# Delta rule: the small products issued in turns over the four quarters of the TensorE array

## The chip, the cores and the metric

One core of one Trainium2 chip runs the whole layer in one program. The metric is the device time of one execution in microseconds; several executions are made, and their median stands for the kernel.

## The reference, cut to what matters

A layer works on 512 latent tokens and 256 context tokens of width 1024. Three mixers read one input projection: a gated linear recurrence, the delta rule (RWKV-7 time mixing) and a neighbourhood attention. Then follow an output projection, a router, and 32 experts of which each token takes 4. The change touches the delta rule alone. It runs in both directions over the tokens, with 4 heads of 64 channels, and carries a 64 x 64 state per head:

```python
def _wkv7_scan(r, w, k, v, a_vec, b_vec, s0, reverse):
    def step(s, inp):
        r_t, w_t, k_t, v_t, a_t, b_t = inp
        sa = jnp.einsum('bhij,bhj->bhi', s, a_t)
        s = s * w_t[:, :, None, :] + sa[..., None] * b_t[:, :, None, :] + v_t[..., None] * k_t[:, :, None, :]
        return s, jnp.einsum('bhij,bhj->bhi', s, r_t)
```

Context tokens come first and give the latent tokens their starting state; only latent tokens give an output.

## The kernel before, in words

The delta rule is computed in chunks of 64 tokens. Six groups g of 128 tokens (two chunks c each) follow one another, g = 0 and 1 over the context, g = 2 to 5 over the latent tokens (`lat`); each is worked for both directions d. A unit is one head of one chunk: ct (2) and h (2) name the head, and a half of the 128 partitions holds one head or one chunk. All products are float32 with 64 rows of contraction and 64 output partitions, so each sits in one quarter of the 128 x 128 array: the half of its contraction rows and the half of its output partitions choose which. Each such product is two instructions on PE in the trace.

`early` (from L505) prepares a group: decays, keys, the products `ba` (L561), then two hops through DRAM and a loop of 15 steps on DVE that inverts the diagonal 16 x 16 blocks (tile M, L607 and L608). At its end it copies M, sends it to DRAM (L613) and reads it back as CX (L616).

`late` (from L621) then does, for one group and direction, a chain of steps with a `yield` after each: `tt` (transposes, L658), twice; `sc` (L672, L673 or L675), twice, once for each h; Y, kv, X, XT, Y, XT (all through `by_chunk`, L651), which complete the inverse of the chunk's matrix; `lv` (L712); `G` (L726 to L732), twice, once for each chunk c; `S` (L755, L757), twice, once for each chunk, which carries the state on. Every step writes one PSUM bank, and DVE or ACT then reads it out (evicts it). The four banks come from one pool that `late` of both directions and `early` share (psE and psR are the same pool of four, L1107). POOL makes X and XT from CX (L644) before the first Y can run.

In G before, a unit's products (3 for the context, 6 for the latent tokens) follow one another in one quarter; then comes the next unit. In `sc`, the two chunks alternate within one h, so two quarters take turns.

The order of the work: `rule` (L1142) takes one step each, in turn, of `late` for both directions and of `early` for the next group. `drive` (L1157) mixes three streams by rounds: two steps of `rule`, one step of `attention` (which starts after 12 idle rounds and has 97 steps left), and 0.22 steps of `modulations` (26 steps: products with the second part of ada_w, and biases). The tile framework then places each instruction on its engine's queue, by this order and by when its planner takes the inputs to be ready; a queue is worked in order. After the rule, `finish` (L767) normalizes its output, and `ahead` (L1177) fills PE with 24 products of the output projection (L1180), which need the attention's PSUM banks and output. Then come the rest of the output projection, the router, and the experts, whose weights stream from HBM.

Of the kernel before, what the change touches and what calls it, by code (L numbers as in the profile page):

```python
# [78 lines left out]
class Mixer:  # L79
# [541 lines left out]
    def late(self, g, d, lp, psR, u, st):  # L621


        nc, ident = self.nc, self.ident
        V, S_, P_, G_ = nc.vector, nc.scalar, nc.tensor, nc.gpsimd
        mm = P_.matmul
        lat = g >= 2
        XA, BK, PC, ba, CX = u['XA'], u['BK'], u['PC'], u['ba'], u['CX']
        bank = lambda nm: psR.tile([128, 512], F32, tag="b", name=nm)
        t_ = lambda nm, shape: lp.tile(shape, F32, tag=nm, name=nm)  # L630
        half = [slice(0, 64), slice(64, 128)]
        hv = lambda ap: ap[:, :256].rearrange("p (u t) -> p u t", u=4)
        units = [(ct * 2 + h, ct, h) for ct in range(2) for h in range(2)]
        TT = t_("TT", [128, 2, 5, 128])
        M3 = t_("M3", [128, 4, 3, 64])
        AM = t_("AM", [128, 2, 4, 64])
        X = t_("X", [128, 4, 64])
        XT = t_("XT", [128, 4, 64])

        def mask(j, msk):  # L640
            G_.tensor_tensor(AM[:, j], ba, msk.unsqueeze(1).to_broadcast([128, 4, 64]), op=ALU.mult)

        def blocks(w, dst):
            G_.tensor_tensor(dst.rearrange("p u (q t) -> p u q t", t=16), CX[:, w].unsqueeze(2).to_broadcast([128, 4, 4, 16]),  # L644
                             self.d16.rearrange("p (q t) -> p q t", t=16).unsqueeze(1).to_broadcast([128, 4, 4, 16]), op=ALU.mult)

        def by_chunk(b, lhsT, rhs, n=64):

            for hu, ct, h in units:
                for c in half:  # L650
                    mm(b[c, hu * n:(hu + 1) * n], lhsT(hu, c), rhs(hu, c), start=True, stop=True)  # L651

        mask(0, self.off16)
        blocks(0, X)
        for ct in range(2):
            b = bank("tt")
            for j, src in enumerate((XA[:, ct, 0, :], BK[:, ct, 0, :], BK[:, ct, 1, :], BK[:, ct, 2, :])):
                P_.transpose(b[:, j * 128:(j + 1) * 128], src, ident)  # L658
            S_.copy(TT[:, ct, 1:5, :], b.rearrange("p (j c) -> p j c", j=4))
            yield  # L660
            if ct == 0:
                blocks(1, XT)
        mask(1, self.off32)

        m3v = M3.rearrange("p (e h) v t -> p e h v t", h=2)
        for h, r in enumerate(half):
            b = bank("sc")
            bv = b[:, :384].rearrange("p (e v t) -> p e v t", e=2, v=3)
            for ct in range(2):
                for c in half:  # L670
                    if lat:
                        mm(bv[c, ct, 0, :], BK[r, ct, 0, c], XA[r, ct, 1, c], start=True, stop=True)  # L672
                        mm(bv[c, ct, 1:3, :], BK[r, ct, 1, c], XA[r, ct, :, c], start=True, stop=True)  # L673
                    else:
                        mm(bv[c, ct, 1, :], BK[r, ct, 1, c], XA[r, ct, 0, c], start=True, stop=True)  # L675
            if lat:
                V.tensor_tensor(m3v[:, :, h], bv, self.m3.unsqueeze(1).to_broadcast([128, 2, 3, 64]), op=ALU.mult)
            else:
                V.tensor_tensor(m3v[:, :, h, 1], bv[:, :, 1], self.m3[:, 1, :].unsqueeze(1).to_broadcast([128, 2, 64]), op=ALU.mult)
            yield  # L680
        b = bank("Y")
        by_chunk(b, lambda hu, c: AM[c, 0, hu, :], lambda hu, c: X[c, hu, :])
        Y = t_("Y", [128, 4, 64])
        S_.copy(Y, hv(b))
        yield
        b = bank("kv")
        by_chunk(b, lambda hu, c: M3[c, hu, 1, :], lambda hu, c: TT[c, hu // 2, 4, half[hu % 2]])
        S_.copy(TT[:, :, 0, :], b[:, :256].rearrange("p (c t) -> p c t", c=2))
        yield
        b = bank("X")  # L690
        by_chunk(b, lambda hu, c: XT[c, hu, :], lambda hu, c: Y[c, hu, :])
        V.tensor_tensor(X, hv(b), X, op=ALU.add)
        yield
        b = bank("XT")
        by_chunk(b, lambda hu, c: Y[c, hu, :], lambda hu, c: XT[c, hu, :])
        V.tensor_tensor(XT, hv(b), XT, op=ALU.add)
        yield
        b = bank("Y")
        by_chunk(b, lambda hu, c: AM[c, 1, hu, :], lambda hu, c: X[c, hu, :])
        Y = t_("Y", [128, 4, 64])  # L700
        S_.copy(Y, hv(b))
        yield
        b = bank("XT")
        by_chunk(b, lambda hu, c: Y[c, hu, :], lambda hu, c: XT[c, hu, :])
        V.tensor_tensor(XT, hv(b), XT, op=ALU.add)
        yield
        LV = t_("LV", [128, 2, 2, 128])
        b = bank("lv")
        bv = b.rearrange("p (c w h i) -> p c w h i", c=2, w=2, h=2)
        for hu, ct, h in units:  # L710
            for c in half:
                mm(bv[c, ct, :, h, :], XT[c, hu, :], TT[c, ct, 0:2, half[h]], start=True, stop=True)  # L712
        S_.copy(LV, b.rearrange("p (c w i) -> p c w i", c=2, w=2))
        yield

        L = t_("L", [128, 2, 2, 64])
        RT = t_("RT", [128, 2, 128]) if lat else None
        G = st['G']
        ys = []
        for c, k in enumerate(half):  # L720
            b = bank("G")
            bv = b.rearrange("p (w e t) -> p w e t", w=4, e=2)
            for ct in range(2):
                for n, h in enumerate(half):
                    hu = ct * 2 + n
                    mm(bv[h, 0, ct, :], LV[k, ct, 1, h], TT[k, ct, 2, h], start=True, stop=True)  # L726
                    mm(bv[h, 1, ct, :], TT[k, ct, 2, h], LV[k, ct, 0, h], start=True, stop=False)
                    mm(bv[h, 1, ct, :], TT[k, ct, 3, h], TT[k, ct, 4, h], start=False, stop=True)
                    if lat:
                        mm(bv[h, 2, ct, :], LV[k, ct, 1, h], M3[k, hu, 0, :], start=True, stop=True)  # L730
                        mm(bv[h, 3, ct, :], LV[k, ct, 0, h], M3[k, hu, 0, :], start=True, stop=False)
                        mm(bv[h, 3, ct, :], TT[k, ct, 4, h], M3[k, hu, 2, :], start=False, stop=True)  # L732
            V.tensor_tensor(G[c], bv[:, 0], self.i2.unsqueeze(1).to_broadcast([128, 2, 64]), op=ALU.add)
            V.tensor_tensor(L[:, c], bv[:, 1], PC[:, :, c:c + 1].to_broadcast([128, 2, 64]), op=ALU.mult)
            if lat:
                V.tensor_tensor(RT[:, :, k], bv[:, 2], XA[:, :, 1, k], op=ALU.add)
                q = (g - 2) * 128 + c * 64
                lo = q if d == 0 else NL - q - 64
                o = self.YD[:, :, lo:lo + 64]
                o = o[:, :, ::-1] if d else o  # L740
                ys.append(o)
                if g < 4:
                    S_.copy(o, bv[:, 3])
                else:
                    V.tensor_tensor(o, bv[:, 3], o, op=ALU.add)
            yield
        for c, k in enumerate(half):
            S, Sn = st['S'][st['n'] % 2], st['S'][(st['n'] + 1) % 2]
            b = bank("S")
            bv = b[:, :256].rearrange("p (w e t) -> p w e t", w=2, e=2)  # L750
            more = not (g == 5 and c == 1)
            for ct in range(2):
                for h in half:
                    if more:
                        mm(bv[h, 0, ct, :], G[c][h, ct, :], S[h, ct, :], start=True, stop=True)  # L755
                    if lat:
                        mm(bv[h, 1, ct, :], S[h, ct, :], RT[h, ct, k], start=True, stop=True)  # L757
            if more:
                for ct in range(2):
                    V.scalar_tensor_tensor(Sn[:, ct, :], bv[:, 0, ct, :], PC[:, ct, c:c + 1], L[:, c, ct, :], op0=ALU.mult, op1=ALU.add)  # L760
            if lat:
                V.tensor_tensor(ys[c], bv[:, 1], ys[c], op=ALU.add)
            st['n'] += 1
            yield
# [1389 lines left out]
```

## Time and profile before

| what | value |
|---|---|
| median of 3 runs | 1767.38 us (1763.82 to 1771.16) |
| the profiled execution, its own time | 1764.35 us |
| its span, first to last instruction | 1762.5 us |
| mean granted TensorE clock | 0.961 of full speed |
| busy, share of the span | PE 92%, PEld 51%, DVE 44%, ACT 28%, POOL 16% |
| data moved by DMA | 508.79 MB, 289 GB/s on average |

PE is the TensorE's products, PEld its weight loads, which overlap them; DVE, ACT and POOL are the vector, scalar and GpSimd engines, SP issues DMAs. Products overlap and their ends are modelled, so a busy PE is not always a PE at its peak. A line such as L726 is a line of the kernel. PEclk is the clock that the chip granted TensorE, 1.00 for 2.4 GHz; its other level is half of that. In rows of waits and in square brackets, `<-` names who released the wait.

### The profile page before, as it was taken

Reading aid. Unit: us, or ns where it says so; the run is one execution under the profiler, and the core shown is the slowest. Engines: PE = TensorE matmul, PEld = TensorE weight load, DVE = VectorE, ACT = ScalarE, POOL = GpSimd, SP = SyncE. Lnnn points to the kernel's source line nnn. Section 1 sums busy time; section 2 is a strip of 40 time slices with the busy share of each in tenths; the row PEclk is TensorE's granted clock in tenths of the full one; section 3 lists DMA queues with packets and bytes.
Section 4 is the critical chain, followed back from the end, with each engine's and each line's share of the span. In section 5 each row is a group of like instructions: output and inputs, shape, how many; then the busy total and the mean of one; then the engine's idle time right before and its main releaser. Section 6 shows DMA issues by size and latency. Waiting matters only on the chain. (4 is left out here: it accounts for less than half of the span.)

```text
span 1762.5 us, 27394 instructions
## 1 busy us (share of the span) xinstructions
PE 1625.5 (92%) x11001; PEld 895.6 (51%) x11001; DVE 773.0 (44%) x1740; ACT 495.0 (28%) x900; POOL 274.7 (16%) x340
## 2 busy tenths in 40 slices
PE   5999986899999979789999999999999999999994
PEld 2778864567778445223543444545435435433352
DVE  6684553577774566112521342536225215211253
ACT  4573321444462225000410221414113113110042
POOL 5100012222330115101111101101111010010101
PEclk9999997899899989899999999999999999999998
DMA  9312446554420767999999999979999999699994
GB/s 308 92 48 86 124 136 134 137 147 130 100 75 15 306 261 300 375 418 412 415 410 408 407 417 349 418 299 397 390 412 410 414 407 421 239 398 375 401 415 142
DMA packets 136273, 508.79 MB, mean 289 GB/s; under 512 B 43153, under 2 KB 58937, under 8 KB 86992
## 3 DMA queue, kind: packets, MB, share of 16 engines
q1 hardware_dynamic: 111916, 470.88, 68.4%
q0 software_dynamic: 21984, 31.78, 7.5%
q10 hardware_dynamic: 2244, 4.34, 0.6%
q8 instruction: 88, 1.44, 0.3%
q14 instruction: 41, 0.34, 0.1%
HBM read 477.47 MB, written 29.47 MB: 288 GB/s over the span
## 5 line engine op out<-in xcount | busy, mean ns | idle before, releaser
L1828 PE MATMUL gu<-w,x 128*64 128x512 f32 (+2 forms) x2432 | 496.5, 604 | 21.7 <-DMA w<-in_moe_w_gu_dram 17.3
L1828 PEld LDWEIGHTS gu<-w,x 128*64 128x64 f32 (+2 forms) x2432 | 151.0, 131 | 311.5 <-issue 291.8
L1841 DVE TENSOR_TENSOR wl<-w,wh 128x1024 fp32r<-128x1024 f32 x144 | 175.5, 1225 | 123.6 <-PE y L1846 66.1
L1828 PE MATMUL y<-w,a 128*32 128x256 f32 (+1 forms) x1536 | 215.6, 489 | 1.0 <-ACT a L1934 1.0
L1840 ACT CAST wh<-w 128x1024 fp32r<-128x1024 f32 x144 | 149.0, 1051 | 184.6 <-PE gu L1844 108.2
L1885 ACT ACTIVATE sg<-gu 128x512 f32<-128x512 f32 (+1 forms) x52 | 28.5, 548 | 514.6 <-PE gu L1828 511.3
L1987 POOL DMA_INDIRECT acc<-ys,gi x31 | 55.6, 1794 | 558.3 <-DVE ys L1985 371.4
L1828 PEld LDWEIGHTS y<-w,a 128*32 128x32 f32 (+1 forms) x1536 | 76.6, 124 | 120.8 <-issue 101.3
L1886 DVE TENSOR_SCALAR sg<-sg 128x512 f32<-128x512 f32 (+1 forms) x52 | 20.8, 400 | 241.0 <-ACT sg L1885 241.0
L1844 PE MATMUL gu<-wh,x 128*128 128x512 f32 x384 | 110.2, 410 | 10.1 <-ACT wh L1840 9.3
L1844 PEld LDWEIGHTS gu<-wh,x 128*128 128x128 f32 x384 | 73.8, 196 | 34.7 <-ACT wh L1840 11.7
L1985 DVE SCALAR_TENSOR_TENSOR ys<-y,got,mod5b 64x512 f32<-64x512 f32 x48 | 36.0, 750 | 124.8 <-PE y L1828 124.5
L1794 POOL DMA_INDIRECT xg<-h2d,gi x42 | 42.9, 1022 | 255.7 <-PE pxt L1816 249.8
L347 PE MATMUL pl<-hh,whi 128*128 128x512 f32 x192 | 78.3, 408 | 0.0
L347 PE MATMUL pl<-hh,wlo 128*128 128x512 f32 x192 | 77.2, 402 | 1.0 <-DVE wlo L327 1.0
L347 PE MATMUL pl<-hl,whi 128*128 128x512 f32 x192 | 76.2, 398 | 0.0
L1517 DVE TENSOR_SCALAR pick<-onesb,sel 96x128 bf16<-96x128 bf16 x32 | 7.9, 249 | 149.6 <-PE y L1944 149.6
L1844 PE MATMUL y<-wh,a 128*128 128x512 f32 x192 | 58.0, 417 | 6.5 <-ACT a L1778 5.7
L1846 PE MATMUL gu<-wl,x 128*128 128x512 f32 x192 | 61.7, 404 | 1.0 <-DVE wl L1841 0.9
L1844 PEld LDWEIGHTS y<-wh,a 128*128 128x128 f32 x192 | 34.8, 188 | 21.2 <-ACT a L1778 7.3
L1928 PEld LDWEIGHTS pat<-ident,act 128*128 128x128 f32 x184 | 26.6, 207 | 34.8 <-issue 32.6
L1846 PEld LDWEIGHTS gu<-wl,x 128*128 128x128 f32 x192 | 37.1, 195 | 10.3 <-DVE wl L1841 1.8
(570 smaller groups left out, 2552.1 us busy)
## 6 DMA issues: line engine op xcount, KB each, us to landing
w<-in_moe_w_gu_dram SPq DMA_DIRECT2D x128, 2048.0 KB
w<-in_moe_w_dn_dram SPq DMA_DIRECT2D x63, 2048.0 KB
aw<-in_ada_w_dram SPq DMA_DIRECT2D x48, 512.0 KB
wraw<-in_w_in_dram SPq DMA_DIRECT2D x11, 1024.0 KB
wo<-in_w_out_dram SPq DMA_DIRECT2D x4, 1024.0 KB
kd<-qk SPq DMA_DIRECT2D x4, 768.0 KB
KT<-kd POOLq DMA_DIRECT2D x8, 384.0 KB
vd<-vt SPq DMA_DIRECT2D x8, 288.0 KB
```

The source lines that it names most:

```text
L347: mm(bl, wt[:, k, :], xx[:, k, NCX:T], start=first, stop=last)
L1794: return self.nc.gpsimd.indirect_dma_start(out=xg, out_offset=None, in_=gv, in_offset=IOA(ap=gi[:xg.shape[0]], axis=0))
L1828: self.nc.tensor.matmul(o, x[0], w, start=False, stop=stop)
L1840: nc.scalar.copy(h, w)
L1841: nc.vector.tensor_tensor(l, w, h, op=ALU.subtract)
L1844: mm(o, y, h[:, c], start=False, stop=False)
L1846: mm(o, xh, l[:, c], start=False, stop=stop)
L1885: nc.scalar.activation(sg, g, AF.Sigmoid, scale=1.702)
L1886: V.tensor_scalar(sg, sg, SIG7, None, op0=ALU.min)
L1928: nc.tensor.transpose(p[:, q * R:(q + 1) * R], acts[x][c_][:, b * 256 + s_:(b + 1) * 256:2], ident[:R, :R])
L1985: V.scalar_tensor_tensor(ys[r], Y[x][0][r], gate[r], mod5b[r, t * w:(t + 1) * w], op0=ALU.mult, op1=ALU.mult)
L1987: nc.gpsimd.indirect_dma_start(out=av, out_offset=IOA(ap=si[:R], axis=0), in_=ys, in_offset=None, compute_op=ALU.add)
```

## The change

Three places in `late`, nothing else. `sc`: both h in one step, on two banks taken at once (one for each h), with the products in turns over the four quarters (c, h); the evictions follow. `G`: both chunks in one step, on two banks taken at once (one for each chunk), each of a unit's 3 or 6 products done for all four (c, h) before the next; the evictions follow. `S`: the products with G for all (ct, h) first, then those with RT. The number of products, their operands and the evictions are the same; `late` has two `yield`s less.

```diff
@@ -663,21 +663,19 @@
-        for h, r in enumerate(half):
-            b = bank("sc")
-            bv = b[:, :384].rearrange("p (e v t) -> p e v t", e=2, v=3)
-            for ct in range(2):
-                for c in half:
-                    if lat:
-                        mm(bv[c, ct, 0, :], BK[r, ct, 0, c], XA[r, ct, 1, c], start=True, stop=True)
-                        mm(bv[c, ct, 1:3, :], BK[r, ct, 1, c], XA[r, ct, :, c], start=True, stop=True)
-                    else:
-                        mm(bv[c, ct, 1, :], BK[r, ct, 1, c], XA[r, ct, 0, c], start=True, stop=True)
+        bs = [bank("sc") for _ in range(2)]
+        bvs = [b[:, :384].rearrange("p (e v t) -> p e v t", e=2, v=3) for b in bs]
+        quarters = [(c, h) for c in range(2) for h in range(2)]
+        for ct in range(2):
+            for j, o, v in ((1, slice(1, 3), slice(0, 2)), (0, 0, 1)) if lat else ((1, 1, 0),):
+                for c, h in quarters:
+                    mm(bvs[h][half[c], ct, o, :], BK[half[h], ct, j, half[c]], XA[half[h], ct, v, half[c]], start=True, stop=True)
+        for h, bv in enumerate(bvs):
             if lat:
                 V.tensor_tensor(m3v[:, :, h], bv, self.m3.unsqueeze(1).to_broadcast([128, 2, 3, 64]), op=ALU.mult)
             else:
                 V.tensor_tensor(m3v[:, :, h, 1], bv[:, :, 1], self.m3[:, 1, :].unsqueeze(1).to_broadcast([128, 2, 64]), op=ALU.mult)
-            yield
+        yield
@@ -717,19 +715,22 @@
+        bs = [bank("G") for _ in range(2)]
+        bvs = [b.rearrange("p (w e t) -> p w e t", w=4, e=2) for b in bs]
+        for ct in range(2):
+            ops = [(0, lambda k, h, hu: (LV[k, ct, 1, h], TT[k, ct, 2, h]), True, True),
+                   (1, lambda k, h, hu: (TT[k, ct, 2, h], LV[k, ct, 0, h]), True, False),
+                   (1, lambda k, h, hu: (TT[k, ct, 3, h], TT[k, ct, 4, h]), False, True)]
+            if lat:
+                ops += [(2, lambda k, h, hu: (LV[k, ct, 1, h], M3[k, hu, 0, :]), True, True),
+                        (3, lambda k, h, hu: (LV[k, ct, 0, h], M3[k, hu, 0, :]), True, False),
+                        (3, lambda k, h, hu: (TT[k, ct, 4, h], M3[k, hu, 2, :]), False, True)]
+            for w, f, first, last in ops:
+                for c, h in quarters:
+                    l, r = f(half[c], half[h], ct * 2 + h)
+                    mm(bvs[c][half[h], w, ct, :], l, r, start=first, stop=last)
         for c, k in enumerate(half):
-            b = bank("G")
-            bv = b.rearrange("p (w e t) -> p w e t", w=4, e=2)
-            for ct in range(2):
-                for n, h in enumerate(half):
-                    hu = ct * 2 + n
-                    mm(bv[h, 0, ct, :], LV[k, ct, 1, h], TT[k, ct, 2, h], start=True, stop=True)
-                    mm(bv[h, 1, ct, :], TT[k, ct, 2, h], LV[k, ct, 0, h], start=True, stop=False)
-                    mm(bv[h, 1, ct, :], TT[k, ct, 3, h], TT[k, ct, 4, h], start=False, stop=True)
-                    if lat:
-                        mm(bv[h, 2, ct, :], LV[k, ct, 1, h], M3[k, hu, 0, :], start=True, stop=True)
-                        mm(bv[h, 3, ct, :], LV[k, ct, 0, h], M3[k, hu, 0, :], start=True, stop=False)
-                        mm(bv[h, 3, ct, :], TT[k, ct, 4, h], M3[k, hu, 2, :], start=False, stop=True)
+            bv = bvs[c]
...
-            yield
+        yield
         for c, k in enumerate(half):
...
-            for ct in range(2):
-                for h in half:
-                    if more:
+            if more:
+                for ct in range(2):
+                    for h in half:
                         mm(bv[h, 0, ct, :], G[c][h, ct, :], S[h, ct, :], start=True, stop=True)
-                    if lat:
+            if lat:
+                for ct in range(2):
+                    for h in half:
                         mm(bv[h, 1, ct, :], S[h, ct, :], RT[h, ct, k], start=True, stop=True)
```

## Rows read from the trace of the kernel before

**Rows 1.** Windows: stretch, us; busy (instructions) of PE, PEld, DVE, ACT, POOL; PEclk; DMA.
```profile
256.20:309.70 53.50, 38.92 (x483) 26.06 (x481) 21.41 (x97) 11.02 (x31) 16.79 (x28) 0.78 0.68 161
309.70:370.30 60.60, 54.74 (x611) 36.06 (x607) 37.24 (x133) 22.52 (x68) 14.79 (x26) 0.92 0.53 135
370.30:429.10 58.80, 57.59 (x765) 43.56 (x764) 44.31 (x139) 23.68 (x74) 16.75 (x29) 0.94 0.57 147
429.10:491.30 62.20, 56.20 (x740) 42.67 (x736) 44.11 (x136) 30.39 (x78) 24.77 (x33) 0.91 0.38 94
491.30:541.60 50.30, 49.63 (x732) 41.09 (x728) 37.88 (x141) 25.88 (x73) 9.87 (x11) 0.97 0.19 59
541.60:570.50 28.90, 28.79 (x569) 24.56 (x566) 10.81 (x40) 6.63 (x14) 3.09 (x5) 1.00 0.10 16
570.50:593.40 22.90, 22.90 (x64) 10.36 (x63) 10.71 (x17) 5.91 (x8) 0.00 (x0) 1.00 0.50 181
...
720.00:1762.50 1042.50, 974.85 (x5304) 428.29 (x5292) 339.44 (x461) 213.52 (x300) 115.69 (x82) 0.97 0.96 382
```

**Rows 2.** Waits of PE, 256.2 to 570.5: us in total, times, longest.
```profile
PE s L901 <- issue: 13.1, 1, 13.1
PE Y L651 <- POOL X L644: 5.1, 2, 4.8
PE o L938 <- ACT pT L926: 4.1, 5, 3.0
```

**Rows 3.** Timeline of PE, the G step of g = 3: start, us, merged runs.
```profile
473.18 0.32 PE L726 MATMUL G<-TT,LV 64*64 64x64 f32 x2
...
473.70 0.27 PE L726 MATMUL G<-TT,LV 64*64 64x64 f32 x1
473.75 0.22 PE L731 MATMUL G<-M,LV 64*64 64x64 f32 x1
...
474.22 0.27 PE L726 MATMUL G<-TT,LV 64*64 64x64 f32 x1
...
474.74 0.27 PE L726 MATMUL G<-TT,LV 64*64 64x64 f32 x1
...
481.63 0.28 PE L732 MATMUL G<-M,TT 64*64 64x64 f32 x2
```

**Rows 4.** Timeline: `ba` over four quarters, two `by_chunk` products over two quarters.
```profile
196.04 0.46 PE L561 MATMUL ba<-XA,BK 64*64 64x64 f32 x16
...
550.92 1.10 PE L651 MATMUL X<-Y,XT 64*64 64x64 f32 x32
551.85 1.10 PE L651 MATMUL XT<-XT,Y 64*64 64x64 f32 x32
```

**Rows 5.** Timeline of PE: first and last of 24 instructions of G, context.
```profile
356.05 0.33 PE L726 MATMUL G<-TT,LV 64*64 64x64 f32 x2
...
356.85 0.28 PE L728 MATMUL G<-TT 64*64 64x64 f32 x2
```

**Rows 6.** Windows of tile sc alone, g = 1 and 5: PE, PEld, DVE.
```profile
309.70:370.30 60.60, 1.58 (x32) 1.17 (x32) 0.95 (x4) 0.92 0.53 135
...
541.60:570.50 28.90, 2.73 (x64) 2.49 (x64) 2.14 (x4) 1.00 0.10 16
```

**Rows 7.** DVE: two of G's evictions; the M loop's operation; one window.
```profile
566.62 0.29 DVE L733 TENSOR_TENSOR G<-G,i 128x128 f32<-128x128 f32 x1 [1.20 <-PE G L732]
566.82 0.28 DVE L734 TENSOR_TENSOR L<-G,PC 128x128 f32<-128x128 f32 x1
...
L607 DVE TENSOR_TENSOR Mt<-P,M x90: 154/202/2050, 210.4 to 539.0; 64x15 f32<-64x15 f32 x12, 64x28 f32<-64x28 f32 x12, 64x39 f32<-64x39 f32 x12, 64x48 f32<-64x48 f32 x12
...
500.00:520.00 20.00, 19.62 (x314) 15.52 (x313) 17.13 (x47) 13.34 (x36) 7.11 (x7) 1.00 0.26 70
```

**Rows 8.** Windows of L1180 (`ahead`) alone: PE and PEld, g = 5 and `finish`.
```profile
541.60:570.50 28.90, 4.69 (x9) 1.38 (x10) 1.00 0.10 16
570.50:593.40 22.90, 18.00 (x40) 7.16 (x39) 1.00 0.50 181
```

**Rows 9.** Timeline of the way from M to Y, g = 5.
```profile
541.16 0.81 SPq L613 DMA_DIRECT2D md<-M  x2
...
545.39 0.72 POOL L644 TENSOR_TENSOR X<-CX,d 128x256 f32<-128x256 f32 x1 [24.76 <-DMA CX<-md]
...
547.53 0.27 PE L651 MATMUL Y<-X,AM 64*64 64x64 f32 x1
```

## The prediction

> **What bounds the kernel now.** First the windows by group of the delta rule [rows 1]: one row for each of its six groups of 128 tokens (g = 0 to 5), then the tail of the rule (`finish`), then the experts. The last row moves weights with the DMA engines busy 96% of the time: from 720 us on, the experts wait for their weights, and those loads start only when the mixers' memory is free and the router has run. So what is won before 593 us moves the whole rest forward, and what is won inside the experts' part would not count. In the rule's rows the reader sees PE busy for nearly the whole of four of six groups (57.6 of 58.8, 49.6 of 50.3, 28.8 of 28.9 us for g = 2, 4, 5), DVE next with 44.3 of 58.8. Second, the waits of PE in this stage [rows 2]: a start-up wait of 13.1 us in g = 0, then little. PE's order of work bounds the stage.
>
> Third, how PE spends it. The timeline of a G step [rows 3] repeats every 0.52 us: one (ct, h) of one chunk, six products of two instructions each, all in one quarter. There are sixteen such blocks for a latent group, 473.18 to 481.63 us, or 8.3 us; a step of one quarter is 0.058 us (two quarters: 0.93 us for 32 instructions from one product to the next [rows 4], 29 ns each, 58 ns per quarter). The block of 12 takes 0.52, not 12 x 0.058 = 0.70, as its end runs beside the next quarter's start. So G uses little over one quarter at a time. `ba` of the same stage [rows 4] already goes in turns over all four quarters and two banks: 16 instructions in 0.46 us, of which the last one's own length is 0.22 [rows 3], so 0.24 for 16, about 15 ns each: four quarters do work at once here.
>
> **The change part by part.** All prices are PE time.
>
> G, latent (g = 2 to 5): the same 192 instructions, at 58/4 = 14.6 ns: 2.8 us in place of 16 x 0.52 = 8.3. Saved 5.5 a group, 22.1 in four. Bounds: nothing (the turns don't overlap), and 5.5.
>
> G, context (g = 0, 1): three products a unit, 24 instructions in about 0.9 us [rows 5], 3.6 us for the 96; after, 96 x 14.6 ns = 1.4. Saved 2.2 a group, 4.5 in two; in g = 0 I count half, as PE there is busy only 38.9 of 53.5 us [rows 1]: 3.3.
>
> sc: the loop already alternates two quarters: 2.73 us for the 64 instructions of a latent group, 1.58 for the 32 of a context group, waits and half-clock included [rows 6]. With four at once half of that: 1.37 saved in each of four latent groups, 5.5; for the context I take half of 32 x 29 ns, 0.46 each, 0.9.
>
> S: 4 instructions per quarter in turns become 2; two quarters were at work before and are after. Nothing, bounds plus and minus 0.3 a group.
>
> Sum on PE: 22.1 + 3.3 + 5.5 + 0.9 = 31.8 us.
>
> Against it stand the waits that the shorter G uncovers. Each G bank is now complete only when its direction's 96 instructions end, and G of the two directions holds all four of the shared banks, as sc does. S needs a bank and G, L, RT out of PSUM. DVE (ACT takes one in four while g < 4) has 16 evictions a group, 0.2 us apart [rows 7]: 3.2 us, begun when the first direction ends; the second's 1.4 us of products cover part. Uncovered 1.8; I take 1.5 in each latent group, 6, and 0.5 in each context group, 1. Upper bound: the 30 operations of the next group's M loop (median 0.2 us, [rows 7]) stand before them on DVE: 6 more a group. The nearest row says they don't all: they were spread over the whole group. Behind a waiting eviction on DVE stand attention's softmax operations; behind a waiting S on PE stands all of attention.
>
> The clock: PE was at the lower of its two levels for 2 x (1 - PEclk) of a window: about 10 us in g = 1, 7 in g = 2, 11 in g = 3, 3 in g = 4, none in g = 5 [rows 1], after waits. More short waits cost perhaps 3 us in all; bounds 0 and 10.
>
> The two removed yields: a `late` has 13 steps in place of 15, so the rule takes 222 turns in place of 246, 111 rounds in place of 123. Attention needs 12 + 97 = 109. It no longer ends 13 rounds ahead of the rule: the last group, which ran alone, gets attention's products beside it. What filled that group, nine instructions of the output product, 4.7 us [rows 8], moves into `finish`, where PE is busy 22.9 of 22.9 us. PE does the same work in another order: nothing, bounds plus and minus 4.7. `modulations` needs 26 turns at 0.22 a round, 118 rounds: only its last two (zeros to memory) come behind the rule; nothing waits for them but a 1 MB load, on SP, that has `finish` as cover.
>
> One step of cover goes with the yields. The next group's M loop ended beside S; now its last step (the copy, then two DMA hops to CX) comes after S. In g = 5 the M loop's DMA went out at 541.16, X was made from CX at 545.39, and Y used it at 547.53 [rows 9], 1.4 us after X was there. From the group's start at 541.6 to Y were 5.9 us of tt and sc [rows 1, 9]; less 1.4 for the shorter sc, but with four or five attention steps now between, that is more than the 5 us from the DMA's issue to X. I take nothing; upper bound in the rivals.
>
> Net: 31.8 - 7 - 3 = about 21 us. Made against the profiled execution's own 1764.35 us that is 1743; the median of the runs shown, 1767.38, stands 3.0 above it, so I say **1746** for the median.
>
> DVE as the cap: g = 2 would need 44.3 us of DVE in 58.8 - 5.4 = 53.4, 0.83; DVE ran at 17.1 of 20 beside a full PE in [rows 7], so this can be.
>
> **The rivals.** (a) *All of it arrives*: waits fall into the shadow of attention, 30 to 33 us gained: 1735. For: g = 4, 5 have PE full to 99%. Against: DVE at 0.83.
>
> (b) *The issue is the floor*: instructions never start closer than the 29 ns seen with two quarters. Then G takes 192 x 29 = 5.6 (2.7 saved), sc 64 x 29 = 1.9 (0.8 saved), context G 2.8 (0.8 saved): 4 x 3.5 + 2 x 0.8 = 16, less 5 of waits: 1756. Against: `ba`, 15 ns [rows 4]. The Trainium skill, TensorE: Matmul & The Clock Gate, section "Wait — 56ns, not 53.3ns?", speaks for it: start to start is said never to fall below about 25 ns however small the product. By that page G would be an estimated 192 x 25 = 4.8 us, and the whole gain some 4 us above (b)'s; the trace of `ba` disagrees with the page, and the trace decides.
>
> (c) *The chain to CX sets the group's length*: if M loop, copy and hops keep their present times, Y of groups 1 to 5 starts no earlier than now, and only the last group's own gain stays, 5.5 + 1.4 = 6.9: 1760, no change that can be told (0.5%, 8.8 us, is about what a measurement of this kernel can tell). For: POOL sat 24.76 us for CX in g = 5 [rows 9]. Against: the hops take 4.2 us, and DVE reaches the M loop earlier when G's evictions come earlier.
>
> (d) *Slower: DVE's queue holds the four banks.* If the M loop's 30 operations stand before G's 16 evictions, S waits 3.2 + 6 + 2 (attention's operations in between) - 1.4 = about 10 us in each of g = 1 to 4: 40, more than the 31.8 saved, and each such wait lowers the clock for what follows (2 us each): 1764 + 40 + 8 - 32, 1780. It decides from 8 us of wait a group. Against: in g = 5, which has no M loop beside it, the evictions follow their products at once [rows 7], and in g = 4 the M loop ended only just before its DMA at 541.16, 0.4 us before the group's end, so it did not run ahead of G. The Trainium skill warns of this side in TensorEngine Tiling (Array Packing), section "PSUM Bottleneck": after a fourfold speedup of TensorE the copies out of PSUM may become the bottleneck. No run here shows it yet.
>
> **How the numbers follow.** Forecast (gain 13 to 29): 0.52. (a) 0.16, (b) 0.10, (c) 0.14, (d) 0.08. Range: below to (a) with 3 us of spread between runs, 1732; above to (c) and a little, 1762; left out are (d) and the edges. Faster by over 0.5%: 0.52 + 0.16 + 0.10 less 0.03 for their edges, 0.75; within: 0.14 + 0.03, 0.17; slower: 0.08.
>
> **What would show it.** Right: a latent group's G, from first start to last, near 2.8 us with its two directions; sc near 1.4; the windows of the latent groups 4 to 7 us shorter each, those of the context groups 1 to 3, the experts' row unchanged in length. Wrong: G's instructions 25 to 29 ns apart (b); new waits of PE at Y for X on POOL, of POOL for CX (c); PE at S waiting for DVE's G, L, RT, with PEclk lower in g = 2 to 4 (d).

## The result, and the profile after

| | before | after |
|---|---|---|
| median | 1765.6 us of 4 runs (1757.84 to 1771.16) | 1744.47 us of 4 runs (1737.1 to 1755.94) |
| profiled execution, its own time | 1764.35 us | 1747.42 us |
| span | 1762.5 us | 1745.6 us |
| mean granted clock | 0.961 | 0.962 |

The ratio is 0.9893, with an interval of 0.9851 to 0.9934: faster by 1.1%, 18.9 us (the two medians are 21.1 us apart). The changed kernel was timed once more beside the experiments below, with the same ratio, 0.9893 (0.9866 to 0.9919). The forecast was 1746.0 us, a gain of 21.

First the windows by group, for the changed kernel: stretch; busy us (instructions) of PE, PEld, DVE, ACT, POOL; PEclk; DMA. They answer to [rows 1].

```profile
256.80:303.60 46.80, 33.81 (x466) 22.84 (x464) 19.85 (x87) 9.48 (x26) 16.79 (x28) 0.78 0.69 172
303.60:367.00 63.40, 51.63 (x601) 34.41 (x598) 34.80 (x126) 20.41 (x63) 15.23 (x26) 0.83 0.45 116
367.00:421.00 54.00, 46.08 (x725) 32.48 (x724) 34.57 (x129) 22.93 (x71) 11.55 (x22) 0.92 0.48 125
421.00:471.30 50.30, 46.46 (x748) 33.36 (x744) 40.51 (x139) 23.41 (x68) 17.70 (x25) 0.97 0.60 153
471.30:521.70 50.40, 42.85 (x736) 33.59 (x733) 42.77 (x136) 31.89 (x75) 23.67 (x24) 1.00 0.31 86
521.70:555.60 33.90, 31.85 (x622) 25.11 (x621) 17.89 (x70) 12.93 (x35) 3.08 (x5) 1.00 0.09 14
555.60:578.50 22.90, 22.90 (x66) 10.53 (x64) 10.41 (x15) 5.15 (x8) 0.00 (x0) 1.00 0.50 171
...
705.20:1745.60 1040.40, 971.72 (x5310) 426.80 (x5300) 339.80 (x461) 213.29 (x300) 115.94 (x82) 0.98 0.96 383
```

The six groups and `finish` took 337.2 us (256.2 to 593.4) and now take 321.7 (256.8 to 578.5): 15.5 of the 16.9 us between the two spans. The experts' stretch has kept its length (1042.5, 1040.4): what is won before it moves it forward. But the gain is spread otherwise than its cause. The groups changed by -6.7, +2.8, -4.8, -11.9, +0.1 and +5.0 us, though every latent group lost the same work. In the last group the reader sees 622 instructions for 569: attention's products now lie beside it. And PE, which was full in g = 2 and 4, now stands for 7.9 us of 54.0 in g = 2 and for 7.5 of 50.4 in g = 4.

The turns themselves are there. The timeline of PE at a G step of g = 3 (start, us, merged runs; compare [rows 3]):

```profile
459.19 0.34 PE L731 MATMUL G<-TT,LV 64*64 64x64 f32 x8
459.36 0.29 PE L731 MATMUL G<-LV,TT 64*64 64x64 f32 x8
459.47 0.30 PE L731 MATMUL G<-TT 64*64 64x64 f32 x8
...
461.92 0.30 PE L731 MATMUL G<-M,TT 64*64 64x64 f32 x8
```

A round of eight instructions over four quarters follows the last after 0.11 to 0.12 us, 14.6 ns an instruction. From the first start of the group's 192 instructions, both directions, to the start of the last eight are 2.73 us (459.19 to 461.92); before, 8.45 us lay between the first start and that of the last two (473.18 to 481.63 in [rows 3]).

The windows of tile sc alone, g = 1 and g = 5 (PE, PEld, DVE; compare [rows 6]):

```profile
303.60:367.00 63.40, 1.36 (x32) 0.95 (x32) 1.04 (x4) 0.83 0.45 116
521.70:555.60 33.90, 1.57 (x64) 1.43 (x64) 2.12 (x4) 1.00 0.09 14
```

For the whole rule (first `tt` to first product of `finish`) the next rows add it up: all tiles, then tile G alone (its 960 instructions and the 176 of S that read G), then sc alone; PE stands first, then PEld, DVE, ACT, and in the first row POOL. Before:

```profile
256.20:571.30 315.10, 286.68 (x3885) 214.28 (x3884) 196.05 (x683) 120.75 (x337) 86.07 (x130) 0.91 0.44 110
256.20:571.30 315.10, 58.87 (x1136) 53.60 (x1136) 17.14 (x72) 2.13 (x8) 0.91 0.44 110
256.20:571.30 315.10, 16.75 (x320) 13.27 (x320) 10.66 (x24) 0.91 0.44 110
```

After:

```profile
256.90:555.90 299.00, 252.87 (x3881) 181.71 (x3880) 190.50 (x683) 121.22 (x337) 88.01 (x130) 0.91 0.45 116
256.90:555.90 299.00, 30.02 (x1136) 24.54 (x1136) 15.71 (x72) 2.13 (x8) 0.91 0.45 116
256.90:555.90 299.00, 9.51 (x320) 8.06 (x320) 10.42 (x24) 0.91 0.45 116
```

PE is busy 33.8 us less (286.68 - 252.87; G 28.9 less, sc 7.2 less). The granted clock of the whole rule is the same, 0.91, but not group by group: g = 1 had 0.83 for 0.92, g = 3 and 4 had 0.97 and 1.00 for 0.91 and 0.97. The rule is only 16.1 us shorter: PE's idle time in it (length less busy) rose from 28.4 to 46.1 us. Where it stands now, the waits of PE in this stage show (us in total, times, longest; compare [rows 2]):

```profile
PE ada L1210 <- DMA aw<-in_ada_w_dram: 11.3, 6, 3.4
PE Y L651 <- POOL X L644: 10.4, 4, 8.7
PE s L904 <- issue: 5.4, 1, 5.4
...
PE S L756 <- ACT yB L744: 2.8, 1, 2.8
PE S L756 <- DVE G L734: 2.6, 2, 1.7
...
PE G L731 <- issue: 2.1, 2, 1.2
PE S L756 <- DVE L L735: 1.8, 1, 1.8
...
PE S L756 <- DVE yB L746: 1.3, 1, 1.3
```

Three kinds are new or have grown. First, `ada` waits for its weights and Y for X: work of PE that outran its transfers. The 8.7 us are in g = 1; the loads of CX and POOL's timeline there (in brackets its idle time and who ended it):

```profile
310.58 1.01 SPq L616 DMA_DIRECT2D CX<-md  x2
...
315.41 1.17 POOL L644 TENSOR_TENSOR X<-CX,d 128x256 f32<-128x256 f32 x1 [2.31 <-DMA CX<-md]
...
325.26 0.73 POOL L644 TENSOR_TENSOR X<-CX,d 128x256 f32<-128x256 f32 x1 [7.81 <-DMA CX<-md]
```

and the same in the kernel before:

```profile
313.58 1.03 SPq L616 DMA_DIRECT2D CX<-md  x2
...
326.53 0.72 POOL L644 TENSOR_TENSOR X<-CX,d 128x256 f32<-128x256 f32 x1 [9.51 <-DMA CX<-md]
...
328.02 0.72 POOL L644 TENSOR_TENSOR X<-CX,d 128x256 f32<-128x256 f32 x1
```

The group began 6.1 us earlier (303.6, before 309.7). The first direction's X came 11.1 us earlier than before, but the second's only 2.8 us earlier (325.26, before 328.02), and for it PE stood. That is rival (c), in one group, with a difference: both loads of CX had gone out 3.0 us earlier than before (310.58, before 313.58), so 3.1 us of cover were lost there, and the second load landed only some 14 us after its issue. What held that transfer the profile does not name.

Second, S waits 8.5 us for evictions of G (2.8 + 2.6 + 1.8 + 1.3). DVE's timeline in g = 4:

```profile
510.34 2.19 DVE L607 TENSOR_TENSOR Mt<-P,M 64x64 f32<-64x64 f32 x1
...
513.77 0.26 DVE L734 TENSOR_TENSOR G<-G,i 128x128 f32<-128x128 f32 x1
...
516.80 0.28 DVE L734 TENSOR_TENSOR G<-G,i 128x128 f32<-128x128 f32 x1
```

and PE's:

```profile
510.07 0.30 PE L731 MATMUL G<-M,TT 64*64 64x64 f32 x8
...
512.16 0.21 PE L731 MATMUL G<-LV,TT 64*64 64x64 f32 x1 [0.86 <-issue]
...
514.77 0.45 PE L756 MATMUL S<-S,G 64*64 64x64 f32 x8 [1.33 <-DVE yB L746]
...
517.13 0.33 PE L756 MATMUL S<-S,G 64*64 64x64 f32 x4 [1.67 <-DVE G L734]
```

By PE's timeline G's first direction was done by 510.4 (its last eight: 510.07); the first eviction began at 513.77, behind steps of the M loop, one of which took 2.19 us. That is rival (d), in small: 8.5 us in the whole rule, not 10 a group.

Third, the row at 512.16 of PE's timeline: within a run of G it stood 0.86 us for nothing that the profile names ("issue"). Such gaps inside G are in every profile with four quarters, and in none of the others (last section).

### The profile page after: what moved, and what is told of

Read it like the earlier page. It is cut to its first block, busy times and chain, and to the rows that moved or that the text cites. A ratio compares the mean times of both kernels' runs of the same rounds, so it can differ in the third digit from the quotient of the medians.

```text
span 1745.6 us, 27396 instructions
## 1 busy us (share of the span) xinstructions
PE 1589.8 (91%) x11001; PEld 863.2 (49%) x11001; DVE 768.2 (44%) x1740; ACT 495.5 (28%) x900; POOL 277.5 (16%) x340
## 5 line engine op out<-in xcount | busy, mean ns | idle before, releaser
L1847 PEld LDWEIGHTS gu<-wh,x 128*128 128x128 f32 x384 | 73.0, 194 | 33.2 <-ACT wh L1843 10.4
L347 PEld LDWEIGHTS pl<-hh,wlo 128*128 128x128 f32 x192 | 36.4, 190 | 10.9 <-DVE wlo L327 1.7
```

The costliest lines, as they stand in the source:

```text
L347: mm(bl, wt[:, k, :], xx[:, k, NCX:T], start=first, stop=last)
L1847: mm(o, y, h[:, c], start=False, stop=False)
```

## The experiments

Each was timed beside the kernel before (medians 1763.37, 1763.57, 1762.07 and 1762.05 us in four sets; the row "changed" is the result above, beside 1765.6). The columns behind the ratio belong to the one profiled execution of each kernel: its span, and of the rule the length, PE's busy and idle time and PEclk. A profile is one run; that of "G alone" lies 7 us under its kernel's median, that of the changed kernel again 7 us over. So times are compared by the ratios, and the split is read for its pattern.

| kernel | median us | ratio (interval) | span | rule | PE busy | PE idle | PEclk |
|---|---|---|---|---|---|---|---|
| before | 1762.1 to 1763.6 | 1 | 1762.5 | 315.1 | 286.7 | 28.4 | 0.91 |
| changed | 1744.47 | 0.9893 (0.9851 to 0.9934) | 1745.6 | 299.0 | 252.9 | 46.1 | 0.91 |
| changed, again | 1746.19 | 0.9893 (0.9866 to 0.9919) | 1751.6 | 305.5 | 257.6 | 47.9 | 0.89 |
| merged steps, no turns | 1755.19 | 0.9960 (0.9936 to 0.9984) | 1753.5 | 304.9 | 272.4 | 32.5 | 0.92 |
| G alone | 1759.37 | 0.9973 (0.9955 to 0.9991) | 1750.2 | 304.9 | 260.8 | 44.1 | 0.90 |
| no idle turns | 1754.12 | 0.9947 (0.9925 to 0.9968) | 1756.2 | 301.7 | 252.7 | 49.0 | 0.88 |
| turns, steps back | 1753.50 | 0.9946 (0.9924 to 0.9967) | 1750.5 | 306.1 | 257.6 | 48.5 | 0.90 |
| idle turns moved | 1749.48 | 0.9904 (0.9873 to 0.9935) | 1748.1 | 302.9 | 259.8 | 43.1 | 0.88 |
| four aw buffers | 1744.65 | 0.9893 (0.9856 to 0.9929) | 1747.5 | 301.1 | 259.1 | 42.0 | 0.88 |
| two quarters | 1744.24 | 0.9899 (0.9861 to 0.9937) | 1739.3 | 293.4 | 258.1 | 35.4 | 0.92 |
| attention later | 1753.82 | 0.9957 (0.9935 to 0.9979) | 1749.7 | 302.1 | 258.5 | 43.6 | 0.89 |
| steps back, attention later | 1745.51 | 0.9903 (0.9872 to 0.9934) | 1744.1 | 297.4 | 254.9 | 42.5 | 0.91 |
| two quarters, attention later | 1751.44 | 0.9944 (0.9922 to 0.9965) | 1744.2 | 296.1 | 263.7 | 32.4 | 0.91 |
| two quarters, steps back, attention later | 1748.15 | 0.9919 (0.9894 to 0.9943) | 1743.8 | 299.6 | 266.5 | 33.1 | 0.91 |

**The changed kernel again**, nothing edited:

> The changed kernel once more, beside the others of this call. Both theories: a ratio to the kernel before of 0.985 to 0.993, and from the first tt to the start of finish about 299 us in place of 314.

0.9893 again, 1746.19 us. The rule of this profile, one of the longer runs, took 305.5 us and not the 299 expected, so one profile can lie 6 us off another of the same kernel.

**Merged steps, no turns.** sc and G keep their single steps on two banks, but each unit's products follow one another in one quarter, as before the change (sc: one h after the other); the loops, shortened:

```diff
-            for w, f, first, last in ops:
-                for c, h in quarters:
+        for c in range(2):
+            for ct in range(2):
+                for h in range(2):
+                    for w, f, first, last in opss[ct]:
```

> The steps, the banks taken at once and the evictions of the changed kernel, but inside each step the order of products of the kernel before: all products of one (ct, h) of one chunk, then the next. Theory P (the gain is PE time, from four quarters at work at once): G of a latent group again takes 8.3 to 8.7 us and sc 2.7, PE's busy time in the rule is within 4 us of before, and the time is within 6 us of the kernel before, or slower by the waits for complete banks. Rival M (the gain is from fewer steps: attention runs beside the last group): about 18 us faster, as the changed kernel.

0.9960, some 7 to 8 us faster than before, though no quarter works beside another that did not before. Neither theory has it: PE's busy time fell by 14.3 us, where theory P had at most 4, and the time by less than half of what rival M had. Its rule, then G and sc alone:

```profile
257.30:562.20 304.90, 272.42 (x3880) 205.24 (x3879) 188.19 (x683) 121.39 (x337) 86.97 (x130) 0.92 0.46 114
257.30:562.20 304.90, 52.60 (x1136) 48.34 (x1136) 16.74 (x72) 2.13 (x8) 0.92 0.46 114
257.30:562.20 304.90, 12.03 (x320) 10.06 (x320) 10.63 (x24) 0.92 0.46 114
```

G and sc, each now issued in one piece, cost 11.0 us less of PE (58.87 to 52.60, 16.75 to 12.03; 2.1 of it are S's instructions that read G, whose order is new too and was not tested by itself). So part of the gain comes with the merged steps, which the prediction put at nothing. At equal steps the turns are worth the rest: 0.9960 to 0.9893, 0.67%, some 12 us. In the two profiles they took 19.6 us off PE (272.42 to 252.87), and PE's idle time rose by 13.6.

**G alone in turns** (sc and S in their old order, sc in its two steps):

> G of the changed kernel, sc and S of the kernel before. Theory P: 25 of the 32 us of PE time saved come from G, so PE's busy time in the rule falls by about 26 us and the time by 12 to 16 us, if the same share of it arrives (17 of 33). Rival M: one of the two removed steps, so half of the gain, about 9 us.

0.9973, under 5 us: a miss for both theories. PE's time is there, 260.8 us, but idle time is 44.1 us. More than half of the saving of G, which by PE's time is the bulk of the change, comes back as waits in this profile (25.9 us less busy, 15.7 more idle).

**Turns, steps back.** The two yields are put back as empty steps (246 turns again):

```diff
@@ after the evictions of sc
         yield
+        yield
@@ after the evictions of G
         yield
+        yield
```

> The changed kernel with one empty step after sc and one after G, so that the rule takes its 246 turns again: turns over the quarters without the fewer steps. If the gain is made of two parts, PE time (9 us beyond the run with the steps merged and no turns, which gained 8) and fewer steps (8), then about 9 us faster than the kernel before, 1754, with attention ending ahead of the last group again. If only the PE time counts: 17 us faster. If the turns are worth nothing without the fewer steps: within 4 us of the kernel before.

0.9946, 9.5 us, as the first of the three cases had it: the turns by themselves at the old number of steps. Its interval and the changed kernel's do not meet. From both sides, then, the turns are worth 10 to 12 us and the fewer steps 7 to 9, with attention let in at round 12. Neither partner without turns was run with another round.

**Two quarters.** Merged steps; G goes in turns over the two h of a chunk, chunk by chunk, and sc one h after the other:

```diff
-            for w, f, first, last in ops:
-                for c, h in quarters:
+        for c in range(2):
+            for ct in range(2):
+                for w, f, first, last in opss[ct]:
+                    for h in range(2):
```

> Steps, banks and evictions of the changed kernel; G's products in turns over two quarters only (the two h of one chunk), sc in the order of the kernel before. On PE, G takes 29 ns an instruction, 5.6 us a latent group for 8.4 and 2.8, so PE's busy time in the rule lies about 16 us under the kernel before's beyond what the merged steps alone gave, near 262 us. If time follows PE beyond the merge: 8 + 0.5 x 9 = 12 to 13 us faster than the kernel before. If the last half of PE's saving only turns into waits: as the changed kernel, 17 us faster.

0.9899: the whole gain. Its rule, then G and sc alone:

```profile
256.80:550.20 293.40, 258.05 (x3880) 190.29 (x3879) 186.35 (x683) 121.05 (x337) 87.22 (x130) 0.92 0.48 118
256.80:550.20 293.40, 38.08 (x1136) 33.51 (x1136) 16.53 (x72) 2.12 (x8) 0.92 0.48 118
256.80:550.20 293.40, 12.04 (x320) 10.06 (x320) 10.64 (x24) 0.92 0.48 118
```

and a piece of G in PE's timeline, 29 ns an instruction:

```profile
452.58 0.28 PE L735 MATMUL G<-LV,TT 64*64 64x64 f32 x4
452.69 0.28 PE L735 MATMUL G<-TT 64*64 64x64 f32 x4
```

G and sc take 10.6 us more of PE than in the changed kernel (38.08 - 30.02, 12.04 - 9.51), and PE's idle time is 10.7 us less (35.4, 46.1). The waits of S on G's evictions are down to 1.0 us. By the times, the first doubling, from one quarter to two, brought all; by the profiles, the second brought PE time that came back as waits.

**One wait at a time.** Three runs each went for one of the new waits. "No idle turns" (WAITP 2 to 0) lets `early` reach the M loop, and so CX, two turns sooner; "idle turns moved" puts these two turns behind the CX loads; "four aw buffers" gives `ada` four buffers for two.

```diff
-WAITP = 2
+WAITP = 0
```

> The changed kernel with the two idle steps of early ahead of the M loop taken out (WAITP 0 for 2), so that the chain M, DRAM, CX stands as far ahead of the next group's Y as it did before the change, or further. Theory W (of the waits that the change uncovered, those of Y for CX and X came from the step of cover that was lost): PE's waits at Y for POOL X fall from 10.4 us to under 4, and the kernel is 4 to 8 us faster than the changed one. Rival: CX is late because its DMA waits behind other transfers, not because of the step: the waits stay, and the time is within 4 us of the changed kernel.

```diff
-        for _ in range(WAITP):
-            yield
...
             res[(g, d)]['CX'] = CX
+        for _ in range(WAITP):
+            yield
```

> The changed kernel with the two idle steps of early moved from ahead of the M loop to the end of early: the chain M, DRAM, CX comes two steps sooner, and the number of turns stays 222, so that attention ends where it does in the changed kernel. Theory W: Y's waits for POOL X fall from 10 us to under 4 and the time falls by 4 to 8 us against the changed kernel, 1738 to 1742. Rival: the wait is taken over by another (S for evictions, as the M loop now stands before them on DVE), and the time is within 4 us of the changed kernel.

```diff
-        aw2 = self.pool(sW, name="aw2", bufs=2, side="right")
+        aw2 = self.pool(sW, name="aw2", bufs=4, side="right")
```

> The changed kernel with four buffers in place of two for the loads of modulations, so that a step's two loads go out a step sooner. Theory: PE's waits for these loads (11 us in the changed kernel, 3 before the change) are uncovered by the change and hold back attention and the rule behind them; they fall under 3 us, and the kernel is 6 to 10 us faster than the changed one, about 1738. Rival: other waits take their place, or the earlier loads delay CX on the DMA engines: within 4 us, with Y's waits longer.

Each shortened its wait: Y for X fell from 10.4 us to 4.2 and 5.2 (under 4 was expected), and with four buffers `ada` has no wait left in the list. None gained. With no idle turns the rule has 212 turns, 106 rounds, fewer than attention's 109; attention ran on into `finish`, which took 31.3 us for 23.1, and the time is 8 us worse than the changed kernel's. Moving the turns gave 1749.48, no better than the changed kernel. With four buffers other waits stand in the list of PE:

```profile
PE s L904 <- issue: 11.1, 1, 11.1
PE Y L651 <- POOL X L644: 6.6, 3, 3.7
PE G L731 <- ACT LV L711: 5.9, 1, 5.9
```

In all three PE's idle time stays at 42 to 49 us, and PEclk is 0.88 where the changed kernel had 0.91 and 0.89.

**Where attention is let in.** The first score product has the longest single wait before (13.1 us, [rows 2]) and with the steps back (14.5); in the changed kernel it is 5.4. Could that explain the steps?

```diff
-ATT0 = 12
+ATT0 = 14
```

> The changed kernel with the attention let in two rounds later (ATT0 14 for 12). Its first score product stands still for 5.4 us behind the load of KT, in which PE has nothing else in its order, while the rule has 111 rounds and the attention would end in about 111. Theory A (that stall is real cost, and work put in front of it covers it): the wait of s falls under 2 us, and the time falls by 3 to 5 us against the changed kernel, to about 1741. Theory M (a wait that goes comes back at another place, as it did with the aw buffers and the idle turns): the wait of s falls all the same, PE's idle time in the rule stays at 43 to 48 us, and the time stays within 2 us of the changed kernel's 1744 to 1746.

0.9957 for 0.9893, slower than the changed kernel by 7.6 us in the medians and 11 by the ratios, which neither theory gave. The wait stayed, 4.8 us. So two rounds in the place of attention move the time by about as much as the turns are worth.

With the steps back, and ATT0 = 20:

> The turns over the quarters with the two empty steps per direction and group put back (123 rounds, as in the run with the steps back, 1753.5), and the attention let in at round 20 for 12, so that it ends near round 117. What is asked: why the two empty steps cost 7 to 8 us. Theory A: they cost because the twelve rounds ahead of the attention hold less real work with them, so that PE reaches the first score product earlier and stands 14.5 us there (5.4 us without them); with the attention at round 20 that wait falls under 4 us and the time by 8 to 11 us, to 1743 to 1746. Theory B: they cost because of what they do to the rest of the rule (one more exchange of the streams per step, other waits); then the wait of s falls too but the time stays at 1749 to 1755.

0.9903, the time that theory A gave, but not by its way. The rule, and the waits of PE:

```profile
256.20:553.60 297.40, 254.87 (x3884) 184.04 (x3883) 197.06 (x683) 119.78 (x337) 85.73 (x130) 0.91 0.48 117
```

```profile
PE s L906 <- issue: 11.9, 1, 11.9
PE s L906 <- ACT pe L916: 9.0, 4, 8.2
PE o L943 <- ACT pT L931: 7.2, 4, 5.8
...
PE S L758 <- DVE S L765: 0.7, 1, 0.7
PE S L758 <- DVE G L735: 0.2, 1, 0.2
```

The first score product still stood 11.9 us, so theory A's mechanism has fallen. In all fourteen profiles it started at 283.2 to 286.0 us, whatever the steps and the round: its loads are issued at raised priority (L945) whatever the round, at 263.9 to 268.6 us in all fourteen, and what releases the first product, the profile does not name. More tells the rest of this list: the empty step between G and S has taken the waits of S on evictions from 8.5 to 0.9 us, and the kernel is no faster than the changed one. Attention's own waits stand in their place. As this run also moved attention, it does not test those waits alone.

**Two quarters, attention later** (ATT0 = 14), and **two quarters with the steps back** (ATT0 = 20):

> The products of G over the two halves of one chunk's channels only, then the other chunk (as in the two-quarter run, 1744.2), with the attention let in two rounds later. There the first score product stood 11.5 us. Theory A: the wait falls to about 6 us and the time by about 5 us, to 1738 to 1740, the fastest of all. Theory M: it stays at 1743 to 1746.

> The products of G over two quarters at a time (26 us of PE for G, as in the two-quarter run), with the two empty steps put back and the attention at round 20. Split the profiled rule into PE's work at full clock, half of the time at the lower clock, and PE's idle time: the kernel before 259 + 27 + 28, the changed kernel 226 + 27 + 46, the two-quarter run 234 + 24 + 35, the changed kernel with steps back and attention at round 20 229 + 26 + 43. In every kernel with turns run so far, but for the one on G alone and the one with only the steps back, work and idle time together come to 265 to 272. Theory F (a floor: the rule's chains of other engines and transfers set some 265 to 272 us, and what PE saves below that comes back as waits): work 234 to 239, idle 28 to 36, and the time within 4 us of the changed kernel, 1741 to 1749. Theory A (the waits of S on G's evictions and the work of PE are separate costs; this version has few of the first, as the run with steps back, and the order of two quarters): idle under 28, and 1735 to 1740.

0.9944: again slower for two rounds' delay, neither theory's figure. And 0.9919, with 33.1 us idle: theory F's range, though PE's work there came out over its range, and "work and idle together" (266.5 less 9% of 299.6, plus 33.1: 272.6) just above its band. As one profile stands for each kernel, and some lie several us off their median, the floor of 265 to 272 us is not shown.

What is shown are three pairs, alike but for two or four quarters (in G and in sc): 0.9899 and 0.9893 (merged steps), 0.9944 and 0.9957 (attention two rounds later), 0.9919 and 0.9903 (steps back, round 20). The two differ by 0.1 to 0.2%, once this way and twice that, far inside the intervals. In all three pairs the profile with four quarters has 9 to 13 us more idle time of PE (46.1 and 47.9 against 35.4, 43.6 against 32.4, 42.5 against 33.1). No version was found that is clearly faster than the changed kernel.

## Why the prediction was right, point by point

The forecast was 1746.0 and the result 1744.47. The sum is right, but in part by luck: two of its terms are wrong, and they cancel.

**What bounds: right as far as it went.** PE was full in three groups before (g = 2, 4, 5; the "four of six" of the working has no fourth row, g = 1 and 3 stand at 90%); after, it stands for 46.1 of the rule's 299.0 us. The gain passed whole to the end, as the experts moved forward with it: 15.5 us up to the end of `finish`, 16.9 in the span.

**PE's saving, 31.8 us: right, 33.8.** G fell by 28.9 us where 25.4 were counted, sc by 7.2 where 6.4 were, and G's latent step came out near the 2.8 us of the working (its 473.18 to 481.63 for the step before are 8.45 us, not the 8.3 of sixteen blocks, which changes little). What was read from `ba`, that four quarters work at once, held. But the run without turns shows that 11.0 us of the two tiles' saving came with merging the steps, which the working does not have; the turns alone took 25.1. So this term, too, has the right size for a cause that is in part another.

**Against it, 10 us: too small.** The working has 7 us of waits and 3 of clock. PE's idle time rose by 17.7 us and the clock in the rule stayed at 0.91 (g = 1 lost what g = 3 and 4 won). The waits on evictions that were named came to 8.5 us against the 7 taken, but waits of `ada` for its weights (11.3 for 2.6 before) and of Y for X (10.4 for 5.1) came beside them, which were put at nothing. With the extra step of the run with attention at round 20 the eviction waits were nearly gone (0.9 us) and nothing was gained. So the waits are no terms that simply add up: each that was taken away was replaced. The step that failed: only the evictions got a price for waits, 7 us, while PE's waits in the whole stage grew by 17.7. Whether the other chains set a limit near here is not shown.

**The removed yields at nothing, plus and minus 4.7: wrong, 7 to 9 us.** That is the other wrong term, outside its bounds. It hid the first: without the yields' share the turns bring 10 to 12 us, where the sum has 21. Why fewer steps gain is only in part known. PE's time for G and sc fell when each was issued in one piece. But with the steps back and attention at round 20 the same time was reached, and in the changed kernel two rounds' delay of attention cost 7.6 to 11 us; so the way in which the streams interleave is worth as much. One row carries a part: PE's stops for "issue" (last section) come to 7.0, 4.0 and 6.6 us with no idle turns, steps back and attention later, and to 1.3 to 2.6 in the kernels with all turns that lost nothing clear. But with two quarters the delay cost some 8 us (the two intervals overlap) without any such stop. The rest is open, and so is what the turns would be worth had attention been moved in the kernel before as well.

**Attention beside the last group: right.** It has 622 instructions for 569, and `finish` two more of the output product (66 for 64, 23.1 us for 22.2), inside the bounds given.

**One lost step of cover for CX, nothing: wrong in g = 1**, where the second direction's X came 2.8 us earlier for a group that began 6.1 us earlier, and PE stood 8.7 us; the other waits of this kind come to 1.7 of the 10.4 us.

**The rivals.** (a) did not come: 33.8 us were saved on PE, 16.1 reached the rule's end. (b) is refuted: instructions start 14.6 ns apart, half of its floor. The Trainium skill, TensorE: Matmul & The Clock Gate, section "Wait — 56ns, not 53.3ns?", has a floor of about 25 ns from start to start; this case's trace disagrees. (c) came true in one group, (d) as 8.5 us in all and not as 40. The Trainium skill, TensorEngine Tiling (Array Packing), section "PSUM Bottleneck", says that copies out of PSUM may become the bottleneck after a fourfold speedup. This case's trace agrees in that the waits of S on evictions rose from nothing in the list before to 8.5 us, and to 1.0 with two quarters; that they set the time is not borne out, by the run in which they fell to 0.9 us.

**The signs named in advance.** G near 2.8 us: seen. sc near 1.4: 1.57 in g = 5 (the 1.36 above is a context group, with half of the instructions). The experts' row unchanged: seen. Latent groups each 4 to 7 us shorter, context groups 1 to 3: not seen group by group (-4.8, -11.9, +0.1, +5.0; -6.7, +2.8); the borders moved with attention's work. The two signs against, waits at Y and at S, were both seen, though of g = 2 to 4 PEclk was lower in g = 2 alone (0.92 for 0.94).

## What to carry to other kernels

Small products that use a quarter of the array can gain from turns, but all of it may come with the first doubling, as here: try two quarters, and read whether PE's idle time grows by what its busy time loses. Where streams are mixed by turns, a change in the number of steps moves every later instruction: here that alone was worth 7 to 9 us, so compare orders of products at equal numbers of steps. A saving on the busiest engine can come back as waits, here 17.7 of 33.8 us. Bound it for the whole stage: three waits that were shortened one by one gave no time back.

## What had not been expected of the hardware

With four quarters PE stops inside its own runs of products: within G it stood for "issue" 2.1 us in the changed kernel (2 gaps, longest 1.2), 6.6 with attention later (3 gaps), 7.0 with no idle turns (3 gaps, longest 4.9). All nine profiles with four quarters have such gaps, of 1.0 us or more in sum; the kernel before, the merged steps without turns and the three kernels with two quarters have none in the list.

The traces show where. In the nine, PE stands 18 times for 0.8 us or more with neither a semaphore to wait for nor a releaser: 17 times inside G, and 2.9 us before a product of attention in the run with the steps back. Count PE's recorded instructions from the start of the program (weight loads, products, semaphore instructions), and each of the 18 stops comes after 5,825, 7,361, 7,617, 8,897 or 10,177 of them: all nine profiles stop at the last, six at 8,897. These numbers differ by multiples of 256, whatever product stands there. So the place in PE's list of instructions decides, and not the data. That the instructions arrive in blocks of 256, which four quarters use up too fast, would explain it; no run tests that.

One step of the M loop took 2.19 us where its median is 0.2 [rows 7]; POOL worked on a 32x1024 tensor (L1508, 510.32 us, 2.13 us) in the same moment. It is not alone: in the rules of the kernel before and of the changed kernel, 15 instructions of DVE took over 0.7 us longer than the median of their line and shape, and all 15 overlap a tensor operation of POOL, though POOL was at such work for only 21 to 22% of the time. The twelve other traces have 80 more in the rule, each beside an instruction of POOL. That POOL's work holds DVE up is thereby likely but not shown; no run moved it away.
